# Retention: the left-over keys' low parts behind the corner scores, the first head's key copies outside of the scores, the second copy of high parts on ScalarE

## The chip, the cores and the metric

The kernel runs on one core of a Trainium2 chip. A core has a matrix engine (TensorE; PE in the profile, with its weight loads PEld), a vector engine (VectorE, DVE), an engine for activations (ScalarE, ACT), a general one (GpSimd, POOL) and a queue engine (SyncE, SP). They run side by side and wait for each other by semaphores. The metric is the time of one execution on the device in microseconds.

## The reference

One transformer block in float32 on 512 tokens of width 1024, with 16 learned tokens (`meta`) put in front, so 528 positions: a feed-forward part, a mixer and a second feed-forward part, each on an RMS-normed input and added to the residual. The mixer projects the input to everything it needs at once, and adds a retention branch (4 heads, keys of 256, values of 512) and an attention branch (8 heads that attend to 128 keys picked by an index score), each with its own gate. The retention, which the change is about, multiplies scores by a decay that depends on the distance of query and key:

```python
inner = jnp.einsum('bhqk,bhke->bhqe', jnp.einsum('bhqd,bhkd->bhqk', qc, kc) * d_in, vc)
cross = jnp.einsum('bhqd,bhde->bhqe', qc, state) * xi
state = g_chunk * state + jnp.einsum('bhkd,bhke->bhde', kc * zeta, vc)
```

In the reference it runs in chunks of 128 with a state. The kernel computes the same as one causal product over all 528 positions.

## The kernel before

Every large product is float32 carried by three products of rounded parts: an operand is split in a high part (a rounded copy, made by ScalarE) and a low part (what is left, a subtraction on VectorE), and high x high, high x low and low x high are added up in PSUM. `in_two` makes the high part at once and returns a function that makes the low part later, so the program decides where in VectorE's queue it stands. Weights (`raw`) become `whi` and `wlo` in the same way.

The order of the work of PE, ScalarE and VectorE is written out by hand here: each engine executes its instructions in the order in which the Python code issues them, and a waiting instruction holds up all behind it on its engine. Tiles come from pools with a fixed number of places (four places for `tmp`); a new tile takes a place whose former reader may still be at work, and then its first write waits for that reader.

The retention of a head h: `decayed(h)` scores all queries against four blocks of 128 keys (`psst`, kb = 0 to 3; PE), multiplies each by the decay (L1837: VectorE, from PSUM to `tmp`) and splits it in `ph` and `pl`. Queries start at position 16 and keys at 0, so the last 16 queries of each block of 128 also meet 16 keys beyond that block of keys, the left-over keys: these small squares of scores are the corners. `corner_keys()` copies those keys next to each other (L1826, two VectorE copies to a `tmp` tile, "CAST" in the profile), `corners(h)` has PE score them in six small matmuls, multiplies them by the decay (L1854), and places the result in `ptail` three times: the high part (L1860, ScalarE), the low part (L1861, VectorE), and the high part again (L1862, GpSimd). The left-over keys' values stand in `vtail` in the same way: `split_last(h)` makes the high parts on ScalarE (L1635 or L1638) and returns the function of the low part (L1639, VectorE). `weigh(h, b)` then adds up for each block of queries the weighted values of all key blocks (`pspv`, L1874), and in one further matmul those of the left-over keys (L1875, called the tail matmul here).

Head 0 runs between gate and query projections: its scores follow the second gate tile, and the corners stand inside the projection of head 1's queries (`psrq`), at its fifth of eight steps. `split_last(0)` and its low part are issued at the second step. Heads 1 to 3 run inside the output projection of the head before (`psro`, `outputs`, four steps of two halves): step 0 splits the left-over values' high parts, step 1 makes their low part and the values' own parts (`values_in`: high by ScalarE, two low parts by GpSimd, L1774), step 2 runs the scores, step 3 the corners between its halves, and then the weighing. Copies of `psro` go through ScalarE (L2019, L2022), and from head 2 on GpSimd adds them up (L2023).

Of the kernel before, what the change touches and what calls it, by code (L numbers as in the profile page):

```python
# [11 lines left out]
F32 = mybir.dt.float32  # L12
F32R = mybir.dt.float32r
AF = mybir.ActivationFunctionType
# [69 lines left out]
def kernel(ctx: ExitStack, tc: tile.TileContext, x, meta, g1, wg1, wu1, wd1, gm,  # L84
                      w_in, w_ro, w_ao, w_mo, g2, wg2, wu2, wd2, gf, rope, decay, causal, out):
    nc = tc.nc
# [1596 lines left out]
    if True:  # L1683
# [145 lines left out]
        def decayed(h):  # L1829
            rk, u = ret_k, heads[h]["u"]  # L1830
            prob, low = [], lambda: None
            for kb in range(4):
                n = S - kb * P
                ps = sm_tile("psst")[:, :n]
                scored(ps, [[t[:, kb * P : (kb + 1) * P] for t in rk[k]] for k in range(2)], lambda t: t[:, kb * P :])
                t = tmp()[:, :n]
                TT(t, ps, u[0][:, :n], ALU.mult)  # L1837
                low()
                ph = rt.tile([P, n], F32R, tag=f"ph{kb}", name="ph")
                pl = rt.tile([P, n], F32R, tag=f"pl{kb}", name="pl")  # L1840
                low = in_two(t, ph, pl)
                prob.append((ph, pl))
                if kb == 1:
                    corner_keys()
            low()
            heads[h]["prob"] = prob

        def corners(h):

            last_k, u = corner["k"], heads[h]["u"]  # L1850
            ps = sm_tile("psst")[:NT, :NT]
            scored(ps.rearrange("p (b q) -> p b q", q=NM), [[last_k[:, 2 * j + i].rearrange("p b q -> p (b q)") for j in range(2)] for i in range(2)], lambda t: t.rearrange("p (b q) -> p b q", q=P)[:, :, P - NM :])
            t = tmp()[:NT, :NT]
            TT(t, ps, u[1], ALU.mult)  # L1854
            last = tp["p"].rearrange("p (a b q) -> p a b q", a=2, q=P)
            for a in range(2):
                at = slice(a * 2 * NM, (a + 1) * 2 * NM)
                src = t[at, at].rearrange("p (b q) -> p b q", q=NM)
                h_, l_, again = (last[i * 2 * NM : (i + 1) * 2 * NM, a, :, P - NM :] for i in range(3))
                nc.scalar.activation(h_, src, AF.Copy)  # L1860
                TT(l_, src, h_.bitcast(F32), ALU.subtract)  # L1861
                nc.gpsimd.tensor_copy(again, h_.bitcast(F32))  # L1862

        def weigh(h, b):

# [40 lines left out]
        def fetch_turned(h, half):  # L1906
            t = heads[h]["land", half] = room4("land")
            nc.sync.dma_start(t.rearrange("p a b -> p (a b)").rearrange("p (k e) -> p k e", k=4),
                              ots[h % 2, half].rearrange("(k p) a e -> p k (a e)", p=P))
# [62 lines left out]
        def queries_keys(h, asides, inside=((), (), (), ())):  # L1972

            pss = {}
            ropes = heads[h]["ropes"] = {}

            def q0(ps):
                pss["qa"] = ps
                asides[0]()

            def q1(ps):
                pss["qb"] = ps
                ropes["q"] = rope_pieces(pss["qa"], ps, cos[:, REAL], sin[:, REAL], S, ret_q)
                asides[1]()
                some(ropes["q"], 5)

            def k0(ps):
                pss["ka"] = ps
                asides[2]()
                some(ropes["q"], 2)  # L1990

            def k1(ps):
                ropes["k"] = rope_pieces(pss["ka"], ps, cos, sin, T, ret_k)
                asides[3]()

            return (steps_of(tiles(("rq", h), w_in, OFF_RQ + h * DK, 2), [proj("psrq", REAL, inside[0], q0), proj("psrq", REAL, inside[1], q1)])
                    + steps_of(tiles(("rk", h), w_in, OFF_RK + h * DK, 2), [proj("psrk", None, inside[2], k0), proj("psrk", None, inside[3], k1)]))

        def outputs(h, beside):

            def step(i):
                def run(w, lower):
                    if h == 0 and i == 0:
                        ixs.close()
                        ap = mx["acc"] = accs.enter_context(pool("acc", 1, side="right"))
                        acc_r.extend(ap.tile([P, S], F32, tag=f"accr{c}", name=f"accr{c}") for c in range(KD))
                        vr["pool"] = vrs.enter_context(pool("vraw", 1, side="right"))
                    if i == 0 and h + 1 < RH:
                        fetch_head(h + 1)
                        new_decay(h + 1)  # L2010
                    elif i == 0:
                        vr["raw"] = fetch_values(0, vraw()[:, :1024])
                    for j in range(2):
                        ps = sm_tile("psro")
                        mm3([(ps, slice(0, S))], [t[:, :, j * P : (j + 1) * P] for t in w],
                            lambda k: [t[:, k, :] for t in heads[h]["o"]], DV // P)
                        a = acc_r[2 * i + j]
                        if h == 0:
                            nc.scalar.activation(a, ps, AF.Copy)  # L2019
                        else:  # L2020
                            t = RR[:, j * S : (j + 1) * S]
                            nc.scalar.activation(t, ps, AF.Copy)  # L2022
                            nc.gpsimd.tensor_tensor(a, a, t, ALU.add)  # L2023
                        if j == 0:
                            lower()
                            if i == 3 and h + 1 < RH:
                                corners(h + 1)
                            beside(i)
                    if h + 1 < RH:
                        if i == 0:  # L2030
                            heads[h + 1]["last"] = split_last(h + 1)
                        if i == 1:
                            heads[h + 1]["last"]()
                            values_in(h + 1)
                        if i == 2:
                            decayed(h + 1)
                        if i == 3:
                            weigh_all(h + 1)
                return run

            return steps_of(tiles(("ro", h), w_ro[h * DV : (h + 1) * DV, :], 0, 4, DV // P, 2 * P), [step(i) for i in range(4)])
# [72 lines left out]
        gr = tiles("gr", w_in, OFF_GR, 7)  # L2114
        more = steps_of(gr[:2], [start_0, start_1])
        nothing = lambda: None
        more += queries_keys(1, (beside_q0, beside_q1, lambda: fetch_turned(0, 1), nothing), (((1, lambda: split_last(0)()), (4, lambda: corners(0))), (), ((3, lambda: (index_queries(4), index_keys(2))), (5, first_pairs)), ((6, pair),)))
        come = [(i, lambda half=half: arrived(0, (half,))) for half, i in enumerate((1, 5))]
        more += steps_of(gr[2:4], [proj("psgate", REAL, (*come, *((i, pair) for i in (2, 4, 6, 7))), later_gate(2)),
                                   proj("psgate", REAL, tuple((i, pair) for i in (1, 3, 5, 6, 7)), after_3)])  # L2120
# [922 lines left out]
    pair = []  # L3043
# [83 lines left out]
```

## Time and profile before

| what | us |
|---|---|
| median of 3 runs (lowest to highest) | 1493.6 (1492.47 to 1494.25) |
| the profiled execution | 1492.96 |
| its span, from first to last instruction | 1491.2 |
| PE busy | 1463.7 (98%) |
| VectorE busy | 1164.0 (78%) |
| ScalarE busy | 784.1 (53%) |
| GpSimd busy | 296.9 (20%) |

How to read the rows shown below. A row of the timeline has the start in us from the span's start, the duration in us, the engine, the line of the kernel, the operation, what it writes and reads, the shape, the number of instructions merged, and in brackets how long the engine stood idle before it and what ended that. A row of the waits has the waiting engine and line, what it waited for, the total in us, how many times, and the longest. A row of the groups has the busy time in us, and the mean of one instruction in ns. A row of the windows has a stretch, its length, the busy time of PE, PEld, DVE, ACT and POOL in it with the number of instructions, the clock granted to TensorE (1.00 is full speed), the share of the DMA engines, and GB/s. An instruction's duration can hold a wait for something that both it and another engine use, since such a wait comes after its start.

### The profile page before, as it was taken

Reading aid. Unit: us, or ns where it says so; the run is one execution under the profiler, and the core shown is the slowest. Engines: PE = TensorE matmul, PEld = TensorE weight load, DVE = VectorE, ACT = ScalarE, POOL = GpSimd, SP = SyncE. Lnnn points to the kernel's source line nnn. Section 1 sums busy time; section 2 is a strip of 40 time slices with the busy share of each in tenths; the row PEclk is TensorE's granted clock in tenths of the full one; section 3 lists DMA queues with packets and bytes.
Section 4 is the critical chain, followed back from the end, with each engine's and each line's share of the span. In section 5 each row is a group of like instructions: output and inputs, shape, how many; then the busy total and the mean of one; then the engine's idle time right before and its main releaser. Section 6 shows DMA issues by size and latency. Waiting matters only on the chain.

```text
span 1491.2 us, 22544 instructions
## 1 busy us (share of the span) xinstructions
PE 1463.7 (98%) x8626; PEld 1291.2 (87%) x8626; DVE 1164.0 (78%) x1702; ACT 784.1 (53%) x1122; POOL 296.9 (20%) x381
## 2 busy tenths in 40 slices
PE   9999999999999999989989999999999999999998
PEld 8999999999988888777878788888888888888887
DVE  5998898866887987478788798889657787767676
ACT  6656465454354554556444547777534644434344
POOL 1101111102111000321142532444202321211110
PEclk9999999999999999999999999999999999999999
DMA  5458787556554452744436343866746576466423
GB/s 172 111 155 198 181 186 190 142 132 228 199 168 144 163 169 112 228 140 157 124 121 202 95 156 97 232 173 177 247 154 228 155 236 202 130 209 189 136 77 122
DMA packets 210333, 247.36 MB, mean 166 GB/s; under 512 B 32208, under 2 KB 153928, under 8 KB 210224
## 3 DMA queue, kind: packets, MB, share of 16 engines
q1 hardware_dynamic: 171824, 179.77, 37.8%
q0 software_dynamic: 34480, 59.30, 16.3%
q10 hardware_dynamic: 3920, 6.84, 1.4%
q8 instruction: 68, 1.11, 0.3%
q14 instruction: 41, 0.34, 0.1%
HBM read 206.47 MB, written 39.21 MB: 165 GB/s over the span
## 4 chain that ended last, share of the span: by engine, by line
PE 92%; DVE 3%; DMA 2%; ACT 1%; issue 1%; ACTq 0%; DVEq 0%; SPq 0%; POOL 0%; POOLq 0%
PE psd L2852 8%; PE psvX L1445 7%; PE psqX L2685 7%; PE psqX L162 7%; PE psqZ L162 5%; PE psd L162 4%; PE psqY L2685 4%; PE psvY L1445 4%; PE psro L162 3%; PE psak L162 3%; PE psrk L162 3%; PE psaq L162 3%; PE psga L162 3%; PE psat L162 3%; PE psmo L162 3%; PE psgate L162 3%
## 5 line engine op out<-in xcount | busy, mean ns | idle before, releaser
L330 DVE TENSOR_TENSOR wlo<-raw,whi 128x1024 fp32r<-128x1024 f32 (+2 forms) x138 | 159.3, 1156 | 36.3 <-ACT whi L329 35.2
L329 ACT ACTIVATE whi<-raw 128x1024 fp32r<-128x1024 f32 (+2 forms) x138 | 130.0, 943 | 84.2 <-PE psat L162 9.4
L330 DVE TENSOR_TENSOR wlo<-w,whi 128x1024 fp32r<-128x1024 f32 x96 | 116.9, 1219 | 62.2 <-ACT whi L329 62.0
L329 ACT ACTIVATE whi<-w 128x1024 fp32r<-128x1024 f32 x96 | 101.6, 1058 | 103.1 <-PE psd L2852 39.3
L162 PE MATMUL psro<-o,whi 128*128 128x512 f32 x256 | 83.3, 408 | 0.0
L329 ACT ACTIVATE whi<-wsum 128x1024 fp32r<-128x1024 f32 (+1 forms) x48 | 48.3, 1007 | 39.7 <-issue 11.8
L119 ACT ACTIVATE whi<-raw 128x1024 fp32r<-128x1024 f32 (+1 forms) x43 | 43.7, 1016 | 36.2 <-PE psat L162 9.1
L120 DVE TENSOR_TENSOR wlo<-raw,whi 128x1024 fp32r<-128x1024 f32 (+1 forms) x43 | 52.7, 1228 | 9.7 <-ACT whi L119 9.5
L162 PEld LDWEIGHTS psro<-o,whi 128*128 128x128 f32 x256 | 50.1, 199 | 10.3
L2648 POOL DMA_DIRECT2D hts<-cross x40 | 26.1, 660 | 165.1 <-DVE cross L2645 144.1
L2852 PE MATMUL psd<-wlo,hh 128*128 128x512 f32 (+1 forms) x148 | 56.7, 383 | 0.0
L2852 PE MATMUL psd<-whi,hl 128*128 128x512 f32 (+1 forms) x148 | 56.7, 383 | 0.0
L2852 PE MATMUL psd<-whi,hh 128*128 128x512 f32 (+1 forms) x148 | 56.7, 383 | 0.0
L330 DVE TENSOR_TENSOR wlo<-wsum,whi 128x1024 fp32r<-128x1024 f32 (+1 forms) x48 | 55.2, 1152 | 1.4 <-ACT whi L329 1.0
L162 PE MATMUL psro<-o,wlo 128*128 128x512 f32 x128 | 51.8, 404 | 0.0
L2023 POOL TENSOR_TENSOR accr<-accr,RR 128x512 f32<-128x512 f32 x24 | 35.6, 1488 | 71.9 <-ACT RR L2022 71.8
L1445 PE MATMUL psvX<-wlo,th 128*128 128x512 f32 x120 | 46.8, 390 | 0.0
L1445 PE MATMUL psvX<-whi,tl 128*128 128x512 f32 x120 | 46.7, 389 | 0.0
L1445 PE MATMUL psvX<-whi,th 128*128 128x512 f32 x120 | 46.7, 389 | 0.0
L162 PE MATMUL psqX<-xh,wlo 128*128 128x264 f32 x144 | 40.9, 284 | 1.1 <-DVE wlo L330 1.1
L162 PE MATMUL psqZ<-xh,wlo 128*128 128x264 f32 x144 | 40.8, 283 | 0.0
L162 PE MATMUL psqX<-th,whi 128*128 128x264 f32 x144 | 40.8, 283 | 0.0
(635 smaller groups left out, 5048.8 us busy)
## 6 DMA issues: line engine op xcount, KB each, us to landing
w<-in_w_in_dram SPq DMA_DIRECT2D x40, 512.0 KB, 4.6
raw<-in_w_in_dram SPq DMA_DIRECT2D x27, 512.0 KB, 3.9
raw<-in_w_in_dram SPq DMA_DIRECT2D x13, 1024.0 KB, 6.1
raw<-in_ffn_w_down_dram SPq DMA_DIRECT2D x24, 512.0 KB, 4.2
raw<-in_ffn_w_up_dram SPq DMA_DIRECT2D x11, 1024.0 KB, 5.3
raw<-in_ffn_w_gate_dram SPq DMA_DIRECT2D x10, 1024.0 KB, 5.4
ws<-in_ffn_w_up_dram POOLq DMA_DIRECT2D x20, 512.0 KB, 6.2
w<-in_ffn_w_up_dram SPq DMA_DIRECT2D x20, 512.0 KB, 5.4
```

The lines of the kernel that those rows point to most:

```text
L119: nc.scalar.activation(hi, src, AF.Copy)
L120: eng.tensor_tensor(lo, src, hi.bitcast(F32), ALU.subtract)
L162: nc.tensor.matmul(o, a[:, k, :], b[:, sl], start=first and k == 0 and i == 0, stop=last and k == nk - 1 and i == 2, skip_group_check=onto)
L329: nc.scalar.activation(hi, src, AF.Copy)
L330: return lambda: nc.vector.tensor_tensor(lo, src, hi.bitcast(F32), ALU.subtract)
L1445: nc.tensor.matmul(d[bank_][t], a, b[:, k, :], start=not onto and j + k + m == 0, stop=j + k == 3 and m == 2, skip_group_check=onto)
L2023: nc.gpsimd.tensor_tensor(a, a, t, ALU.add)
L2648: nc.gpsimd.dma_start(d.rearrange("(b i) a e -> a i b e", i=32)[a], cross[32 * a : 32 * a + 32].rearrange("p b c t -> p b (c t)"))
L2685: nc.tensor.matmul(ps[:, t], a, b[:, k, :], start=not onto and j + k + m == 0, stop=j + k == 3 and m == 2, skip_group_check=onto)
L2852: nc.tensor.matmul(ps, a, m[:, j, cs], start=first and i == 0, stop=last and i == 2)
```

## The change

Three edits, all in the retention's bookkeeping of the left-over keys. What is computed stays the same.

```diff
@@ decayed(h)
                 prob.append((ph, pl))
-                if kb == 1:
+                if kb == 1 and h:
                     corner_keys()
@@ corners(h)
                 nc.scalar.activation(h_, src, AF.Copy)
+                nc.scalar.activation(again, src, AF.Copy)
                 TT(l_, src, h_.bitcast(F32), ALU.subtract)
-                nc.gpsimd.tensor_copy(again, h_.bitcast(F32))
+            heads[h].pop("last")()
@@ outputs(h, beside), step i
                         if i == 1:
-                            heads[h + 1]["last"]()
                             values_in(h + 1)
@@ the query projection of head 1, steps 1 and 4 of its first tile
-((1, lambda: split_last(0)()), (4, lambda: corners(0)))
+((1, lambda: (corner_keys(), heads[0].update(last=split_last(0)))), (4, lambda: corners(0)))
```

First, head 0's keys are copied after all its scores, no longer between the second and the third block. Second, the copy of the high part that GpSimd made from ScalarE's first copy is made by ScalarE from the source. Third, the low part of `vtail` is made at the end of `corners(h)`, in head 0 too. From L1861 on, lines after the change have a number that is one higher.

VectorE in head 0, from the second block's product on: the piece of the difference around the scores.

```order
 L1837 TENSOR_TENSOR tmp<-psst,RR 128x384
 L330 TENSOR_TENSOR pl<-tmp,ph 128x512
-L1826 CAST tmp<-rqk 128x4x48
-L1826 CAST tmp<-rqk 128x4x16
 L1837 TENSOR_TENSOR tmp<-psst,RR 128x256
 L330 TENSOR_TENSOR pl<-tmp,ph 128x384
```

The two copies of the keys no longer stand ahead of the third block's product (128x256). They come behind the values' second low part:

```order
 L330 TENSOR_TENSOR pl<-tmp,ph 128x128
 L1774 TENSOR_TENSOR vl<-vl,vh 128x1024
+L1826 CAST tmp<-rqk 128x4x48
+L1826 CAST tmp<-rqk 128x4x16
+L1854 TENSOR_TENSOR tmp<-psst,ulast 64x64
+L1862 TENSOR_TENSOR ptail<-tmp,ptail 32x2x16 x2
 L1639 TENSOR_TENSOR vtail<-vtail 32x1024
-L1854 TENSOR_TENSOR tmp<-psst,ulast 64x64
-L1861 TENSOR_TENSOR ptail<-tmp,ptail 32x2x16 x2
```

Here the corners' product and low parts also changed places with the low part of `vtail`. VectorE in head 1, whose scores begin behind a weight's low part (`wlo`) and a selection step (MAX, MATCH_REPLACE); heads 2 and 3 read the same:

```order
 L1599 MAX top<-score_6522 128x8
 L1600 MATCH_REPLACE score_6522<-top,score_6522 128x512
-L1639 TENSOR_TENSOR vtail<-vtail 32x1024
 L330 TENSOR_TENSOR wlo<-raw,whi 128x1024
 L1837 TENSOR_TENSOR tmp<-psst,RR 128x512
...
 L1854 TENSOR_TENSOR tmp<-psst,ulast 64x64
-L1861 TENSOR_TENSOR ptail<-tmp,ptail 32x2x16 x2
+L1862 TENSOR_TENSOR ptail<-tmp,ptail 32x2x16 x2
+L1639 TENSOR_TENSOR vtail<-vtail 32x1024
```

The low part left its place ahead of `wlo` and the scores and stands behind the corners' low parts, as the last thing that the tail matmul needs. The order of PE's instructions and of the loads issued by SyncE is unchanged.

## Prediction before the result

> **What bounds the kernel now.** I read the page's first part and its chain, then TensorE's (PE's) own waits.
>
> ```profile
> span 1491.2 us, 22544 instructions
> PE 1463.7 (98%) x8626; PEld 1291.2 (87%) x8626; DVE 1164.0 (78%) x1702; ACT 784.1 (53%) x1122; POOL 296.9 (20%) x381
> PE psst L1818 <- DVE tmp L1837: 11.0, 3, 4.5
> PE pspv L1875 <- POOL ptail L1862: 6.7, 1, 6.7
> ```
>
> PE sets the time, so work elsewhere counts only where PE waits. It waits in two places worth anything, both in the retention, both touched by the change: once 6.7 us in the first head (head 0), and three times, 11.0 us together, in heads 1 to 3. Each wait costs twice, as the stretches with their granted clock show (start:end, length, busy us of PE, PEld, DVE, ACT, POOL, then PEclk).
>
> ```profile
> 182.42:185.83 3.41, 2.31 (x20) 2.10 (x18) 1.97 (x3) 1.06 (x1) 0.00 (x0) 1.00 0.68 114
> 704.65:708.06 3.41, 0.64 (x6) 0.64 (x6) 3.18 (x3) 2.03 (x4) 1.03 (x1) 1.00 0.00 0
> 708.06:711.48 3.42, 3.42 (x11) 2.74 (x10) 2.72 (x9) 2.07 (x4) 0.00 (x0) 0.50 0.00 0
> 637.96:643.21 5.25, 5.25 (x12) 4.12 (x13) 2.62 (x5) 1.49 (x4) 0.13 (x1) 0.50 0.01 4
> 769.50:776.33 6.83, 5.73 (x17) 4.77 (x18) 5.90 (x12) 2.72 (x5) 2.81 (x2) 0.50 0.00 1
> 834.36:837.77 3.41, 3.41 (x10) 2.65 (x9) 3.13 (x8) 1.28 (x3) 0.69 (x1) 0.50 0.84 289
> ```
>
> After each long wait PE runs at half clock for 3.4 or 6.8 us; half of PE's busy time there is lost: 2.6, 1.7, 2.9, 1.7 us. A stretch of 3.41 us with PE idle for 1.1 of it (182.42) was followed by no slow one; one with 2.77 idle (704.65) was.
>
> **Head 0: the keys copied later.** Before, in order of time:
>
> ```profile
> 624.50 0.39 DVE L1826 CAST tmp<-rqk 128x192 fp32r<-128x192 f32 x2
> 627.26 0.43 PE L1818 MATMUL psst<-rqk,tmp 128*64 128x64 f32 x5
> 627.77 0.43 DVE L1837 TENSOR_TENSOR tmp<-psst,RR 128x256 f32<-128x256 f32 x1 [2.88 <-PE psst L1818]
> 630.65 2.00 ACT L1784 ACTIVATE g<-g 128x1024 f32<-128x1024 f32 x2
> 632.56 1.04 ACT L329 ACTIVATE whi<-raw 128x1024 fp32r<-128x1024 f32 x1
> 633.61 2.12 ACT L1638 ACTIVATE vtail<-vtail 32x1024 fp32r<-32x1024 f32 x2
> 635.76 1.22 DVE L1639 TENSOR_TENSOR vtail<-vtail 32x1024 fp32r<-32x1024 f32 x1 [4.32 <-ACT vtail L1638]
> 637.01 0.22 DVE L1854 TENSOR_TENSOR tmp<-psst,ulast 64x64 f32<-64x64 f32 x1
> 637.96 0.80 PE L1875 MATMUL pspv<-vtail,ptail 96*128 96x512 f32 x1 [6.71 <-POOL ptail L1862]
> ```
>
> The third product with the decay (627.77) starts only when the corner matmuls that read the copied keys are through: its `tmp` takes the place of that copy. ScalarE's whole row of work, up to the high parts of the left-over keys' values (ending 635.73), hangs behind it. With the copy after the scores, the product starts where the CAST stood, near 624.5. I take 3.2 us of the 3.27 for all of ScalarE's row, as nothing in it is shown waiting for a load. From the end of `vtail`'s high parts to PE's tail matmul it was 2.23. Now it is the four small copies and their low parts (about 1.0, priced below), then the low part of `vtail`, 1.22: the same 2.2, since the corner product (0.22) now lies ahead of ScalarE's copies. The tail matmul starts near 634.75: **3.2 earlier**. The two CASTs now follow four small products and low parts and one `vl`, together about 3.2 us, so the corner matmuls wait to about 628.2, 1 us later than before. That is hidden: PE still reaches the tail near 632.1 and waits there until 634.75. Without that cover it would cost 1 us.
>
> **Heads 1 to 3: the low part moved.** Head 1:
>
> ```profile
> 699.92 2.41 POOL L1774 TENSOR_TENSOR vraw<-vraw,vh 128x1024 fp32r<-128x1024 f32 x1 [13.50 <-ACT vh L1771]
> 702.31 3.37 POOL L1774 TENSOR_TENSOR vraw<-vraw,vh 128x1024 fp32r<-128x1024 f32 x1
> 700.58 2.84 DVE L1639 TENSOR_TENSOR vtail<-vtail 32x1024 fp32r<-32x1024 f32 x1
> 703.62 3.15 DVE L330 TENSOR_TENSOR wlo<-raw,whi 128x1024 fp32r<-128x1024 f32 x1 [0.20 <-DVE vtail L1639]
> 705.44 0.58 ACT L2019 ACTIVATE accr<-psro 128x512 f32<-128x512 f32 x1
> 707.40 0.63 ACT L329 ACTIVATE ph<-tmp 128x512 fp32r<-128x512 f32 x1 [1.38 <-DVE tmp L1837]
> 707.42 0.33 PE L1818 MATMUL psst<-rqk 128*128 128x128 f32 x1 [3.08 <-DVE tmp L1837]
> 711.35 1.23 DVE L330 TENSOR_TENSOR wlo<-raw,whi 128x1024 fp32r<-128x1024 f32 x1 [0.66 <-ACT whi L329]
> 716.37 0.40 PE L1875 MATMUL pspv<-vtail,ptail 96*128 96x512 f32 x1
> ```
>
> The low part takes 1.22 in head 0 and 2.84 here, `wlo` 1.23 or 3.15. The ends say why: the low part ends 1.1 after the first GpSimd subtraction, the second one ends 2.26 after the low part, `wlo` 1.1 after that. Two engines take turns here, one instruction at a time. Without the low part, `wlo` takes its turn (702.25 to 703.45), and the score product that frees PE's bank follows at 703.4, not 706.7, if it need not take turns itself:
>
> ```profile
> 768.82 2.26 POOL L2023 TENSOR_TENSOR accr<-accr,RR 128x512 f32<-128x512 f32 x1
> 769.86 0.68 DVE L1837 TENSOR_TENSOR tmp<-psst,RR 128x512 f32<-128x512 f32 x1
> 771.03 1.28 POOL L2023 TENSOR_TENSOR accr<-accr,RR 128x512 f32<-128x512 f32 x1
> 771.24 1.61 DVE L330 TENSOR_TENSOR pl<-tmp,ph 128x512 fp32r<-128x512 f32 x1 [0.23 <-ACT ph L329]
> L1837 DVE TENSOR_TENSOR tmp<-psst,RR 128x512 f32<-128x512 f32 x4 | 2.7, 682 | 2.2 <-PE psst L1818 2.2
> ```
>
> It does not: 0.68 beside a GpSimd addition, and 682 ns is the mean of all four. `pl`, with both inputs in SBUF, does (1.61).
>
> So PE's wait of 3.08 at 707.42 and its slow stretch go. But they don't all become time: what was moved is late next. ScalarE's `ph` can't start before its copy ends at 706.02, so the run from `ph` to the end of the second `wlo` (707.40 to 712.58, 5.18) ends at 711.2. Behind it stand the corner product (0.22), the four copies with their low parts (1.0) and now the moved low part (1.22): the tail's operand is ready near 713.6. PE, at full clock from 704.34, needs 716.37 - 707.42 - 1.7 = 7.25 and is there at 711.6. New wait 2.0; the tail starts at 713.6 instead of 716.37, **2.8 earlier**.
>
> Heads 2 and 3 differ: GpSimd also has two additions of 1.28 queued behind its subtractions, and DVE's keys' CASTs come now between them.
>
> ```profile
> L1826 DVE CAST tmp<-rqk 128x192 fp32r<-128x192 f32 x4 | 1.0, 252 | 0.0
> L1826 DVE CAST tmp<-rqk 128x64 fp32r<-128x64 f32 x4 | 0.8, 191 | 0.0
> L1860 ACT ACTIVATE ptail<-tmp 32x32 fp32r<-32x32 f32 x8 | 1.8, 229 | 2.0 <-DVE tmp L1854 1.9
> 772.78 0.35 DVE L1826 CAST tmp<-rqk 128x192 fp32r<-128x192 f32 x2
> 835.52 0.35 DVE L1826 CAST tmp<-rqk 128x192 fp32r<-128x192 f32 x2
> 780.64 0.40 PE L1875 MATMUL pspv<-vtail,ptail 96*128 96x512 f32 x1
> 842.25 0.40 PE L1875 MATMUL pspv<-vtail,ptail 96*128 96x512 f32 x1
> ```
>
> No row shows a CAST beside a GpSimd instruction, so its price is between 0.35 and 0.35 + 2 x 1.28 for the pair. It takes 61 ns for 128 more elements, where the product takes 682 for 512: a faster way of running, so I price it like the nearest row that waits, `pl`, as taking turns: the pair then ends near 772.1 in head 2 (before 773.1) and 835.0 in head 3 (before 835.9). The corner matmuls wait about 1.7 in both. Everything behind follows by 1.0 and 0.9 earlier, then the low parts meet one more addition, and the low part of `vtail` ends near 778.6 and 841.4: tails **2.0** and **0.85 earlier**. If CASTs don't take turns, each is 1.5 better.
> [...]
>
> **The second copy.** Eight GpSimd copies go, eight on ScalarE come, 0.23 each by the L1860 row (the same shape and source); the 0.5 per head is inside the 1.0 above. They delay ScalarE's next copy of `psro`, which waits for PE anyway. The low part delays one selection step by 1.2 us on DVE; its next job waits for PE's first weighted sum.
>
> **The sum.** Tails: 3.2 + 2.8 + 2.0 + 0.85 = 8.85. Clock: the losses of heads 1 to 3 lie before their tails and are in these; head 0's 2.6 lies behind its tail and goes too. Against that stand the new waits ahead of the four tails, 2.0 to 2.75 us: between the 1.1 that cost nothing and the 2.77 that did, nearer to the latter. Each may cost 0 to 1.7; I take 1.0, so 4.0. Net 8.85 + 2.6 - 4.0 = 7.4. The profiled execution took 1492.96, its span and 1.76 around it; so 1485.5 for it, and 1486 beside the median of 1493.6.
>
> **Rivals.**
> *No new slow stretch*, because a wait must fill a whole 3.4 us: the 4.0 falls away, 1482. For it: 1.1 us idle cost nothing. Against it: 2.77 of 3.41 sufficed.
> [...]
> *CASTs take no turns*: 3.0 better, 1483.
> *The stall merely moves in heads 1 to 3*: if the chain to the low part ends where PE arrived before (2.8, 2.0, 0.85 later than I work out, say through more turns lost to additions), only 3.2 + 2.6 - 4.0 = 1.8 is left: 1491.8, no change. For it: the low part is now the last link of its chain in every head.
> *Head 0's edit does nothing*, because the third product waits for another reader of `tmp`: 5.65 - 3.0 = 2.7, 1491. Against it: the 2.88 ends exactly with the corner matmuls.
> *Slower, by the clock*: one long stall becomes two shorter ones (seven in all: corner and tail in heads 0, 2 and 3, the tail in head 1). If 1 to 1.7 us idle is enough for a slow stretch, and the four long ones give two each as at 769.50, it is 3 x 1.7 + 4 x 2.75 = 16.1 against 11.45: 4.6 slower, 1498. It decides where such a short wait slows PE at all; the 182.42 row, at 1.1, speaks against it.
>
> **How the numbers follow.** Forecast 0.50, no new slow stretch 0.15, CASTs 0.12, stall moves 0.10, head 0 nothing 0.08, slower 0.05. A measurement tells 0.2%, 3.0 us, from no change. Faster: the first three and a few parts of the fifth, 0.80; same 0.15; slower 0.05. The forecast's own range runs from four waits at no cost (1482) to four at 1.7 (1488.8), with 1 us of turns more, 1490. With the cheaper CASTs below and part of the moved stall above: 1480 to 1491.
>
> **What would show it.** Right: PE's wait on L1837 down from 11.0 us to under 2; waits of 2 to 3 us at the tail matmul behind the low part in all heads; the third product of head 0 near 624.5; L1639 at 1.2 us; `ph` in head 1 straight behind a `psro` copy. Wrong: L1837 still late behind a GpSimd subtraction; CASTs at 0.35 beside additions; PE waiting for weights or loads where it did not before; half clock after waits under 1.5 us.

## The result, and the profile after

The changed kernel takes 1483.7 us (median of 6 runs, 1481.85 to 1486.41), beside 1493.03 for the kernel before on the same chip. The ratio is 0.9943, with a 95% interval of 0.9925 to 0.9962: 8.5 us less, 6 to 11 by the interval. The profiled execution is the slowest of the six, 1486.41, with a span of 1484.6. A second profile of the same kernel, taken later beside the experiments, has a span of 1483.9.

The page's first part, after the change:

```profile
span 1484.6 us, 22535 instructions
...
PE 1462.5 (99%) x8626; PEld 1288.9 (87%) x8626; DVE 1155.0 (78%) x1702; ACT 785.5 (53%) x1130; POOL 298.3 (20%) x373
```

PE's waits after the change (engine and line, what ended the wait, total us, times, longest):

```profile
PE pspv L1876 <- ACT RR L2023: 4.3, 2, 2.2
PE pspv L1876 <- POOL bias L1595: 3.0, 1, 3.0
PE psst L1818 <- DVE tmp L1826: 2.7, 3, 1.1
PE pspv L1876 <- ACT accr L2020: 1.8, 1, 1.8
PE psS L2271 <- ACT ak L329: 1.3, 1, 1.3
...
PE psst L1818 <- DVE tmp L1837: 0.5, 1, 0.5
```

The 11.0 us at L1837 are down to 0.5. The 6.7 at head 0's tail matmul became four waits at the tail matmuls (L1876 now), 3.0, 1.8 and twice 2.2: 9.1 together. The names of what ended them mislead: in the timeline the low part of `vtail` (L1639) ends 0.1 to 0.2 us ahead of each tail matmul, later than anything else that it reads.

The timeline of the changed kernel, head 0:

```profile
623.52 0.42 DVE L1837 TENSOR_TENSOR tmp<-psst,RR 128x256 f32<-128x256 f32 x1
...
626.52 0.36 DVE L1826 CAST tmp<-rqk 128x192 fp32r<-128x192 f32 x2
626.94 0.54 PE L1818 MATMUL psst<-rqk,tmp 128*64 128x64 f32 x6 [0.58 <-DVE tmp L1826]
...
629.43 2.13 ACT L1638 ACTIVATE vtail<-vtail 32x1024 fp32r<-32x1024 f32 x2
...
632.35 0.18 DVE L1862 TENSOR_TENSOR ptail<-tmp,ptail 32x32 fp32r<-32x32 f32 x1 [0.32 <-ACT ptail L1860]
632.56 1.22 DVE L1639 TENSOR_TENSOR vtail<-vtail 32x1024 fp32r<-32x1024 f32 x1
...
633.99 0.47 PE L1876 MATMUL pspv<-vtail,ptail 96*128 96x512 f32 x1 [2.98 <-POOL bias L1595]
```

The third product (623.52) no longer has a wait ahead of it, ScalarE's high parts of `vtail` end at 631.55 and not at 635.73, and the tail matmul is now bound by ScalarE's four small copies and VectorE's low parts behind them.

Head 1, and behind it head 2 (whose GpSimd rows at L2024 are the additions):

```profile
700.62 0.58 ACT L2020 ACTIVATE accr<-psro 128x512 f32<-128x512 f32 x1
701.09 1.03 ACT L329 ACTIVATE ph<-tmp 128x512 fp32r<-128x512 f32 x2
...
705.03 1.22 DVE L330 TENSOR_TENSOR wlo<-raw,whi 128x1024 fp32r<-128x1024 f32 x1 [0.66 <-ACT whi L329]
...
707.40 1.22 DVE L1639 TENSOR_TENSOR vtail<-vtail 32x1024 fp32r<-32x1024 f32 x1
...
708.72 0.47 PE L1876 MATMUL pspv<-vtail,ptail 96*128 96x512 f32 x1 [1.83 <-ACT accr L2020]
...
761.62 2.99 POOL L2024 TENSOR_TENSOR accr<-accr,RR 128x512 f32<-128x512 f32 x2
762.15 2.52 DVE L1826 CAST tmp<-rqk 128x192 fp32r<-128x192 f32 x2
...
764.81 0.51 PE L1818 MATMUL psst<-rqk,tmp 128*64 128x64 f32 x6 [1.06 <-DVE tmp L1826]
...
769.64 1.22 DVE L1639 TENSOR_TENSOR vtail<-vtail 32x1024 fp32r<-32x1024 f32 x1
...
770.96 0.69 PE L1876 MATMUL pspv<-vtail,ptail 96*128 96x512 f32 x1 [2.15 <-ACT RR L2023]
```

In head 1, `ph` stands right behind a copy of `psro`, and the low part of `vtail` takes 1.22, where it took 2.84. In head 2 the two CASTs take 2.52 us beside two additions; before they took 0.35.

The granted clock behind the waits, in windows of the changed kernel:

```profile
706.19:709.60 3.41, 1.58 (x8) 1.02 (x7) 2.69 (x8) 1.89 (x6) 0.00 (x0) 1.00 0.00 0
709.60:713.02 3.42, 3.42 (x10) 2.64 (x9) 1.65 (x3) 1.11 (x4) 0.00 (x0) 0.50 0.02 5
...
767.63:771.04 3.41, 1.26 (x7) 0.75 (x6) 3.02 (x6) 1.51 (x5) 2.70 (x2) 1.00 0.01 2
771.04:774.46 3.42, 3.42 (x9) 2.65 (x10) 1.99 (x4) 0.80 (x2) 0.96 (x1) 0.50 0.00 0
829.07:832.48 3.41, 1.50 (x7) 0.92 (x5) 3.05 (x5) 1.64 (x6) 2.49 (x2) 1.00 0.00 0
832.48:835.89 3.41, 3.17 (x14) 2.64 (x15) 2.28 (x6) 1.49 (x4) 1.29 (x1) 1.00 0.00 0
972.43:975.84 3.41, 1.91 (x10) 1.18 (x9) 2.44 (x6) 1.93 (x4) 0.07 (x1) 1.00 0.86 247
975.84:979.26 3.42, 3.42 (x15) 3.16 (x14) 3.42 (x12) 3.37 (x4) 0.51 (x1) 0.50 0.24 85
```

Half clock follows the tail waits of heads 1 and 2 (709.60, 771.04), and likewise that of head 0. It does not follow head 3's wait (832.48) in this profile; in the second one it does, at 832.15. A new half-clock stretch (975.84) lies in the attention, some 140 us behind the last changed instruction.

Where the time went is best seen by cutting the span at PE's own rows. "To the tail" runs from a head's first score matmul (L1818) to its first tail matmul, "weighing" from there to its fourth tail matmul, and "attention" from its first score matmul (`psS`) to its first output matmul (`psmo`); all are us, differences of two starts.

| stretch | before | changed | changed, second profile | only the keys' copies moved | only the low part moved | only the second copy |
|---|---|---|---|---|---|---|
| head 0 to the tail | 17.26 | 14.34 | 14.35 | 14.07 | 18.07 | 18.03 |
| weighing | 9.42 | 8.54 | 8.54 | 8.52 | 8.52 | 8.49 |
| head 1 to the tail | 15.31 | 12.49 | 12.49 | 16.72 | 12.23 | 16.79 |
| weighing | 6.96 | 8.59 | 8.60 | 6.96 | 7.02 | 6.96 |
| head 2 to the tail | 18.30 | 14.64 | 14.69 | 15.66 | 15.91 | 15.93 |
| weighing | 6.96 | 8.57 | 8.58 | 6.96 | 8.57 | 6.96 |
| head 3 to the tail | 15.64 | 14.18 | 14.14 | 15.83 | 14.67 | 15.57 |
| weighing | 6.96 | 7.02 | 8.59 | 6.96 | 7.03 | 6.96 |
| attention | 205.16 | 207.27 | 206.09 | 205.18 | 205.05 | 204.73 |

The tails came 2.92, 2.82, 3.66 and 1.46 earlier, 10.86 in all. A weighing of 8.5 to 8.6 instead of 6.96 is one with a half-clock stretch. The attention, which nothing in the diff touches, took 2.1 and 0.9 us longer in the two profiles of the changed kernel.

The last three columns belong to the experiments. They also show how far one profile can be trusted: in the two kernels that leave the order of VectorE's work in heads 1 and 2 as it was (keys' copies, second copy) head 1 to the tail differs from before by +1.4 and +1.5, and head 2 by -2.6 and -2.4. The double half-clock stretch (6.83 us, at 769.50 before) fell in head 1 and not in head 2, and a turn that VectorE lost to GpSimd ahead of head 2's scores before (a `wlo` of 2.16 us) was not lost there (1.22). Sums over all heads, and the timed ratios, carry the argument.

### The profile page after: what moved, and what is told of

The parts are those of the page before. It is cut to its first block, busy times and chain, and to the rows that moved or that the text cites. A ratio compares the mean times of both kernels' runs of the same rounds, so it can differ in the third digit from the quotient of the medians.

```text
span 1484.6 us, 22535 instructions
## 1 busy us (share of the span) xinstructions
PE 1462.5 (99%) x8626; PEld 1288.9 (87%) x8626; DVE 1155.0 (78%) x1702; ACT 785.5 (53%) x1130; POOL 298.3 (20%) x373
## 4 chain that ended last, share of the span: by engine, by line
PE 88%; DVE 4%; ACT 3%; DMA 3%; issue 1%; POOL 0%; SPq 0%; DVEq 0%; ACTq 0%; POOLq 0%
PE psd L2852 8%; PE psqX L2685 7%; PE psvX L1445 7%; PE psqX L162 7%; PE psqZ L162 5%; PE psd L162 4%; PE psqY L2685 4%; PE psvY L1445 4%; PE psrk L162 3%; PE psat L162 3%; PE psmo L162 3%; PE psak L162 3%; PE psrq L162 3%; PE psdX L162 2%; PE psaq L162 2%; PE psga L162 2%
## 5 line engine op out<-in xcount | busy, mean ns | idle before, releaser
L330 DVE TENSOR_TENSOR wlo<-raw,whi 128x1024 fp32r<-128x1024 f32 (+2 forms) x138 | 154.7, 1123 | 39.6 <-ACT whi L329 38.9
L330 DVE TENSOR_TENSOR wlo<-w,whi 128x1024 fp32r<-128x1024 f32 x96 | 116.8, 1219 | 62.1 <-ACT whi L329 61.9
L162 PE MATMUL psro<-o,whi 128*128 128x512 f32 x256 | 79.4, 391 | 0.0
L330 DVE TENSOR_TENSOR wlo<-wsum,whi 128x1024 fp32r<-128x1024 f32 (+1 forms) x48 | 55.2, 1152 | 1.4 <-ACT whi L329 1.0
L2024 POOL TENSOR_TENSOR accr<-accr,RR 128x512 f32<-128x512 f32 x24 | 37.9, 1581 | 64.1 <-ACT RR L2023 64.0
L162 PE MATMUL psqX<-th,wlo 128*128 128x264 f32 x144 | 40.7, 283 | 0.0
```

The costliest lines, as they stand in the source:

```text
L162: nc.tensor.matmul(o, a[:, k, :], b[:, sl], start=first and k == 0 and i == 0, stop=last and k == nk - 1 and i == 2, skip_group_check=onto)
L330: return lambda: nc.vector.tensor_tensor(lo, src, hi.bitcast(F32), ALU.subtract)
```

## The experiments

### The change once more, and its three parts one by one

The changed kernel again, with no edit:

> The change itself beside its three parts. Theory (the edits act at different places): its gain is the sum of the three parts' within 3 us, 7 to 11 us. Rival (the parts need each other): it gains over 3 us more than their sum.

Measured: 0.9943 (0.9927 to 0.996), the same ratio as at first, 1485.5 us beside 1493.2, some 8.5 us by the ratio and so in the range expected. The stretches to the tails are the same to 0.05 us (the table); the half clock behind head 3's appeared here and not in the first profile.

Only the keys' copies of head 0 moved (against the kernel before):

```diff
-                if kb == 1:
+                if kb == 1 and h:
                     corner_keys()
-((1, lambda: split_last(0)()), (4, lambda: corners(0)))
+((1, lambda: (corner_keys(), split_last(0)())), (4, lambda: corners(0)))
```

> Only head 0's keys are copied after its scores; the low part stays at its old place and GpSimd keeps the second copy. Theory (the third product waited for the corner matmuls through the place in tmp): that product starts some 0.1 us after the first low part, the 6.7 us wait at head 0's tail matmul falls to 3 to 3.5, the 11.0 us at L1837 in heads 1 to 3 stay; 3.2 of the tail and 0 to 1.7 of the clock come off: 2 to 5 us faster than before. Rival (the gain at head 0 needs the low part's move or ScalarE's second copy): the wait stays above 5 us, under 1 us faster.

Measured: 0.996 (0.9945 to 0.9975), 6.0 us, where 2 to 5 were expected. Its PE waits, and the third product:

```profile
PE psst L1818 <- DVE tmp L1837: 10.1, 3, 3.6
PE pspv L1875 <- POOL ptail L1862: 2.7, 1, 2.7
...
624.71 0.42 DVE L1837 TENSOR_TENSOR tmp<-psst,RR 128x256 f32<-128x256 f32 x1
```

The third product starts 3.9 us after the head's first score (620.83), where it started 7.1 after (620.70 and 627.77). Head 0's wait fell from 6.7 to 2.7 (3 to 3.5 expected), its tail came 3.19 earlier (17.26 to 14.07), and heads 1 to 3 kept their 10 us. So the place of a `tmp` tile in head 0, not the values' high parts, held up ScalarE's whole row; the rival that head 0's edit does nothing falls.

Only the low part of `vtail` moved:

```diff
                 nc.gpsimd.tensor_copy(again, h_.bitcast(F32))
+            heads[h].pop("last")()
-                            heads[h + 1]["last"]()
                             values_in(h + 1)
-((1, lambda: split_last(0)()), (4, lambda: corners(0)))
+((1, lambda: heads[0].update(last=split_last(0))), (4, lambda: corners(0)))
```

> Only the low part of vtail is moved behind the corners, in all heads. Theory (the low part cost a turn ahead of the weight's low part and the first product): PE's wait at L1837 falls from 11.0 us to under 2, head 0 keeps its 6.7 us, and the tail matmuls of heads 1 to 3 now wait 1.8 to 2.7 us each; 5.65 us earlier tails less up to 1.7 of slow clock each: 1 to 5.5 us faster. Rival (the stall only moves): waits of 3 us or more at the tails, within 1 us of before.

Measured: 0.9959 (0.9943 to 0.9975), 6.1 us, where 1 to 5.5 were expected. Its PE waits:

```profile
PE pspv L1876 <- issue: 13.2, 4, 7.5
...
PE psst L1818 <- DVE tmp L1837: 1.6, 2, 1.2
```

The wait at the scores fell from 11.0 to 1.6, and the tails' waits in heads 1 to 3 are 1.62, 1.85 and 2.21. In heads 1 and 3 this is all of the change's effect but some 0.5 (12.23 and 14.67 to the tail, beside 12.49 and 14.18). In head 2 the tail came at 15.91 and not 14.64. In head 0 the wait grew from 6.7 to 7.5, but not by the low part's new place: from the end of `vtail`'s high parts to the tail it is 2.1 us, where it was 2.23. A `pl` of VectorE (L330 at 629.71), right behind the third product, took 1.52 beside a GpSimd instruction that had been waiting for a load (L1733 at 629.53); before, the same `pl` took 0.55 and started just ahead of that instruction (628.12 and 628.16).

Only the second copy on ScalarE:

```diff
                 nc.scalar.activation(h_, src, AF.Copy)
+                nc.scalar.activation(again, src, AF.Copy)
                 TT(l_, src, h_.bitcast(F32), ALU.subtract)
-                nc.gpsimd.tensor_copy(again, h_.bitcast(F32))
```

> Only the second copy of the high parts goes from GpSimd to ScalarE. Theory: nothing that PE waits for moves, waits of 11.0 and 6.7 us stay within 0.5, time within 1.5 us of before. Rival (0.5 us more on ScalarE per head is on the path): head 0's wait 0.3 to 0.5 us longer, 0.5 to 2 us slower; rival (GpSimd's copy was the last link, as the wait names it): 0.5 to 1 us faster in head 0.

Measured: 0.9998 (0.9984 to 1.0011). No difference can be measured. PE waits 10.2 us at L1837, and 7.5 ahead of head 0's tail; that is 0.8 more than before, where at most 0.5 was expected, but not by the copies: from the end of `vtail`'s high parts to the tail it is 2.13 beside 2.23, and the same `pl` as in the kernel above lost a turn (1.42). The weighing behind it was 0.9 shorter (8.49 for 9.42), and the two stretches together are no longer than before (26.5 and 26.7).

The parts alone give 6.0, 6.1 and 0.3, 12.4 together, and the change 8.5; the sum was expected to come within 3 us. With intervals of some 2 us on each of the four the gap of 3.9 is not clear of noise, but the two profiles of the change show where such a gap may lie. All three weighings behind the tails of heads 1 to 3 can carry half clock there (1.6 each), where the low part alone shows it once; and the attention lost 0.9 to 2.1 in them alone.

### What the four new waits hang on

Each of the next three kernels adds one edit to the changed kernel. The copies of the keys of heads 1 to 3 by ScalarE:

```diff
+                if h:
+                    nc.scalar.activation(do, of.bitcast(F32), AF.Copy)
+                else:
                     nc.vector.tensor_copy(do, of.bitcast(F32))
```

> The changed kernel, but the copies of heads 1 to 3's keys (the CASTs) are made by ScalarE in place of VectorE; nothing is left out. Theory (a CAST takes 1.3 us in heads 2 and 3 because it takes turns with GpSimd's additions, 1.1 us each, and PE's corner matmuls wait for it): the copies last under 0.4 us beside the additions, PE's corner waits of 1.06 and 1.08 us vanish or fall under 0.4, the two tails start 1 to 2 us earlier, and the time is 1 to 3 us below the changed kernel's, 1481 to 1484.5. Rival (the CASTs are only late, since the scores and their high parts end late): the copies on ScalarE start as late as the CASTs ended, the corner waits stay at 1 us or more, and the time is within 1 us of the changed kernel's.

Measured: 0.992 (0.9905 to 0.9935), 3.4 us better than the change by the ratios, with intervals that just overlap. Head 2 (in this kernel L1827 is the copy, L2027 the additions):

```profile
758.44 0.50 ACT L1827 ACTIVATE tmp<-rqk 128x192 fp32r<-128x192 f32 x2
759.00 3.31 POOL L2027 TENSOR_TENSOR accr<-accr,RR 128x512 f32<-128x512 f32 x2
...
760.99 0.48 PE L1818 MATMUL psst<-rqk,tmp 128*64 128x64 f32 x6
```

The pair takes 0.50 on ScalarE, where it took 2.52 on VectorE, PE no longer waits for the corners, and the tails of heads 2 and 3 come 1.6 and 1.7 earlier (13.06 and 12.49). So the CASTs' turns with GpSimd set the corner waits. The tail waits stayed, at 1.6 to 1.8 in heads 1 to 3.

The corners ahead of the weight's second low part, and the low part of `vtail` ahead of `ptail`'s:

```diff
             TT(t, ps, u[1], ALU.mult)
+            heads[h].pop("last")()
 ...
                 TT(l_, src, h_.bitcast(F32), ALU.subtract)
-            heads[h].pop("last")()
 ...
                         if j == 0:
-                            lower()
                             if i == 3 and h + 1 < RH:
                                 corners(h + 1)
+                            lower()
```

> The changed kernel with the low part of vtail issued right behind the corners' product, ahead of ptail's low parts, and with the corners issued ahead of the weight's second low part (wlo); nothing is left out. Theory (the tail matmul waits because three things in a row end late: wlo 1.2 us, ptail's parts, and vtail's low part 1.2 us): the tail's wait in head 1 falls from 1.8 to under 0.6, in heads 2 and 3 from 2.15 to 1.0 or less, tails of heads 1 to 3 start 1 to 2 us earlier each, one or more of the slow stretches behind them go; 1478 to 1482. Rival (wlo is needed at once by PE): the wait reappears as long in a PE wait for wlo behind the tail or in the projection, and the time stays within 1 us of 1485.

Measured: 0.989 (0.9873 to 0.9907), 7.9 us better than the change. Head 2 (L1863 is `ptail`'s low part here):

```profile
761.76 1.22 DVE L1639 TENSOR_TENSOR vtail<-vtail 32x1024 fp32r<-32x1024 f32 x1
...
763.09 2.34 DVE L1863 TENSOR_TENSOR ptail<-tmp,ptail 32x32 fp32r<-32x32 f32 x2
...
764.27 0.47 PE L1876 MATMUL pspv<-vtail,ptail 96*128 96x512 f32 x1 [0.42 <-ACT RR L2023]
```

The tail's wait is gone in head 1, 0.42 in head 2 and 0.2 in head 3, with no wait for `wlo` in its place; the weighings of heads 1 to 3 are 6.96, 7.02 and 7.02, without half clock. This is the largest gain of the three kernels: ahead of the tail's last links stood `wlo`, which nobody needed yet. Its two moves were not run apart, and a score product in head 3 now waits 1.2 where it did not.

Head 0's gate step (a table load and two activations) behind the corners:

```diff
             heads[0]["low"](1)
-            open_gates(0)
 ...
-(4, lambda: corners(0))
+(4, lambda: (corners(0), open_gates(0)))
```

> The changed kernel with the first head's gate step (a load of the activation table and two ACTIVATEs, 3.3 us of ScalarE) issued behind the corners, no longer ahead of the high parts of vtail; nothing is left out. Theory (ScalarE's row alone sets the end of head 0's tail): the wait of 2.98 us ahead of head 0's tail falls under 0.5, the tail starts 2.5 to 3 us earlier, the slow stretch behind it (1.5 us lost) goes; 4 us below the changed kernel, 1480 to 1482. Rival (VectorE's row sets it: CASTs, corner product, low parts): the wait only falls to 1.5 to 2.5 us and the slow stretch stays; 1484 to 1485.5.

Measured: 0.9922 (0.9906 to 0.9937), 3.1 us better than the change, again with intervals that just overlap. Head 0:

```profile
629.04 1.22 DVE L1639 TENSOR_TENSOR vtail<-vtail 32x1024 fp32r<-32x1024 f32 x1
...
630.61 0.40 PE L1876 MATMUL pspv<-vtail,ptail 96*128 96x512 f32 x1
```

No wait is left ahead of head 0's tail, which comes 3.2 earlier than in the changed kernel (14.34 to 11.16), and its weighing is at full clock (6.83 for 8.54). ScalarE's row alone set that tail.

### All three together, and what is left

The last three edits in one kernel, run twice, on two chips:

> The three edits before together: key copies of heads 1 to 3 on ScalarE, vtail's low part and the corners ahead of wlo, the first head's gate step behind the corners; nothing is left out. Theory (each takes a wait of its own, and the slow stretches go with the waits): no PE wait over 1 us is left in the retention, and the time is the sum of the three, 8 to 12 us below the changed kernel: 1473 to 1478. Rival (the waits are one chain, or the gain goes to another wait in the attention that follows): less than 5 us below, 1481 or more.

> The version with all three edits once more, beside the three runs before it on the same chip. Expected: a ratio of 0.987 to the kernel before, within 0.002, and a profile with the same waits (1.2 twice at the score products); which heads show half clock may differ, since the same wait was followed by half clock in one execution and not in another.

Measured: 0.9868 (0.9851 to 0.9886) and 0.9858 (0.9839 to 0.9878): some 20 us below the kernel before, and faster than the changed kernel by more than the intervals. The longest group of waits in the retention, from the first run (L1840 is the score product):

```profile
PE psst L1818 <- DVE tmp L1840: 2.4, 2, 1.2
```

No wait over 1.2 us is left in the retention (none over 1.0 was expected), and one half-clock stretch, in head 3, behind a window of 3.41 us with waits of 0.3 and 1.2 in it. The edits alone are worth 3.4, 7.9 and 3.1 over the change, 14.4 together; in one kernel they give 11 to 13. Part of this need not be an overlap of the edits: in each of their three profiles the attention takes 204.5 to 205.6 us and in the two of the change 206.1 and 207.3, and that difference counts three times in the 14.4. The next run tests one of the edits for overlap.

The same without the keys' copies on ScalarE:

> The three edits together but without the key copies on ScalarE (they stay on VectorE); nothing is left out. Theory (once vtail's low part stands ahead, the tail no longer hangs on the corners, so a CAST's turn of 1.1 us costs PE only the corner wait of 1.0 in heads 2 and 3): corner waits of about 1.0 and 1.0 return, the waits for the score product (1.2 each) shrink or stay, and the time is within 1.5 us of the version with all three (about 1473). Rival (the gains of the edits add): 3 us above the version with all three, 1476 or more.

Measured: 0.9863 (0.9847 to 0.9879), beside 0.9858 for all three on the same chip: no difference can be measured. In this profile the corner waits of 1.05 and 1.03 are back, and one of the two waits of 1.2 at the score products is gone. Once the tail no longer hangs on the corners, a corner wait of 1 us mostly takes the place of another one.

The weight's low part of the third output step behind the second score product (added to all three):

```diff
                 TT(t, ps, u[0][:, :n], ALU.mult)
+                if kb == 1:
+                    weight()
                 low()
 ...
-                            lower()
+                            if i != 2 or h + 1 == RH:
+                                lower()
                             beside(i)
 ...
-                            decayed(h + 1)
+                            decayed(h + 1, lower)
```

> The version with all three edits, and the weight's low part (wlo) of the third output step issued behind the second score product, no longer ahead of the first; nothing is left out. Theory (the two waits of 1.2 us that are left in heads 2 and 3 are the first product queued behind wlo, which takes turns with GpSimd's subtraction for 2.0 us): both vanish or fall under 0.3, the corner and tail matmuls start about 1 us earlier in heads 2 and 3, and the time falls by 2 to 4 us to 1469 to 1471. Rival (wlo is then late for PE's next output matmuls): a wait of 0.5 to 1.5 us for wlo in heads 1 to 3 takes their place, and the time stays within 1 us or rises.

Measured: 0.9861 (0.9839 to 0.9883), no gain over 0.9858, where 2 to 4 us were expected; the rival had the time right and the wait wrong. The two waits of 1.2 did go, and PE did not wait for `wlo` in the retention, but in head 2 this came instead (L1868 is `ptail`'s low part, L2029 the additions, L1881 the tail):

```profile
760.03 3.32 POOL L2029 TENSOR_TENSOR accr<-accr,RR 128x512 f32<-128x512 f32 x2 [0.90 <-ACT RR L2028]
761.10 2.31 DVE L1868 TENSOR_TENSOR ptail<-tmp,ptail 32x32 fp32r<-32x32 f32 x2
...
762.26 0.47 PE L1881 MATMUL pspv<-vtail,ptail 96*128 96x512 f32 x1 [1.74 <-ACT RR L2028]
```

`ptail`'s two low parts (0.18 each alone, L1862 in head 0 above) took turns with two additions and lasted 2.31, and the tail waited 1.74 again, and 0.98 in head 3.

The same with the keys' copies back on VectorE:

> As the run before, but with the key copies of heads 1 to 3 on VectorE; nothing is left out. Theory (CASTs take turns with the additions, so the corner waits of about 1 us return in heads 2 and 3): 1 to 3 us above the run before. Rival (with the products earlier, the CASTs come before the additions and take no turn): under 0.5 us per pair and the same time as the run before within 1 us.

Measured: 0.9889 (0.9869 to 0.9908), 4.2 us worse than the kernel before it in this list by the two ratios (1 to 3 expected), though the intervals overlap. Head 2:

```profile
757.14 1.41 DVE L1826 CAST tmp<-rqk 128x192 fp32r<-128x192 f32 x2
...
758.70 0.63 PE L1818 MATMUL psst<-rqk,tmp 128*64 128x64 f32 x6 [1.86 <-DVE tmp L1826]
```

Only one CAST of the pair lost a turn here, but the low parts ahead of it had lost theirs (a `wlo` of 2.48 us, a `pl` of 1.77), and the corner waits are 1.86 and 1.69, each followed by half clock. Of the kernels run, the one with all three edits is the best, with the two before this one no different within the noise; the order of VectorE's work beside GpSimd's additions is what is left to arrange.

## Why the prediction was right, point by point

**The sum.** Forecast 1486.0, measured 1483.7; the profiled run was put at 1485.5 and took 1486.41. The time alone does not tell the forecast from the rivals at 1482 and 1483; the profiles do, with slow stretches behind the new waits and CASTs that take turns. The mechanisms are those forecast, but the terms erred in both directions, and that they cancelled is luck. In the profiled spans: tails 10.86 earlier (8.85 predicted); clock -2.42 (0.9 gained in head 0's weighing, 1.63, 1.61 and 0.06 lost in the others; -1.4 predicted from 2.6 and 4.0); the attention and the rest -2.96 (2.11 in the attention; nothing predicted); and 1.06 from a start of the retention that was earlier in this execution. 10.86 - 2.42 - 2.96 + 1.06 = 6.54, the difference of the spans (1491.17 - 1484.63), where 7.4 was predicted. The second profile gives 10.84 - 4.01 - 1.36 + 1.82 = 7.29. The earlier start is not the change's: before, PE waited 1.1 us for a weight at 185.75, more than 430 us ahead of the first changed instruction, and in the two profiles of the change it did not; in the profiles of its three parts it did, 1.1 to 2.1.

**Head 0.** Right in mechanism and size. The third product starts 3.2 earlier once the start's shift of 1.06 is taken off (627.77 to 623.52), and the tail 2.92, not 3.2: the way from the high parts of `vtail` to the tail is 2.44 us (631.55 to 633.99), not 2.2, since the fourth copy and both low parts stand in a row. The corner matmuls' later start (628.0 on the clock of before, predicted 628.2) was hidden, as said. The slow stretch went from 6.8 to 3.4 us, so the clock's net gain of 1.6 (2.6 less 1.0) was 0.9.

**Head 1.** Right to 0.1: counted from the first score the tail comes at 12.49, where the forecast's rows give 12.5 (713.6 - 701.06), and the wait is 1.83 (2.0). That it is 2.82 earlier (2.8) hangs on the one profile before; beside the two other kernels with the old order it is 4.2 and 4.3 earlier, since they had a double half-clock stretch there.

**Heads 2 and 3.** The CASTs take turns, as priced against the cheaper case: 1.34 and 1.26 us beside the additions, where they took 0.18 to 0.26 before. No row of before had a CAST beside a GpSimd addition, so the price, taken from `pl` (1.61), was an estimate. On ScalarE the pair takes 0.50 beside the same additions. Beside the profile before, the sizes were off: the corner waits are 1.06 and 1.08, not 1.7, and the tails 3.66 and 1.46 earlier, not 2.0 and 0.85. The step that was mis-sized is where the pair of CASTs ends. Counted from the head's first score matmul (762.34 before, 756.31 after), head 2's pair ends 2.4 us earlier (773.13 before, 764.66 after), and 1.0 was predicted; from there to the tail it is 6.3, where 6.5 was predicted. I had left GpSimd's additions where they were. But the first one starts 5.3 us after the first score and not 6.5 (768.82 before, 761.62 after), and the CASTs' turns come that much sooner. The cause lies further back, 12.5 us ahead of head 2's scores, in a `wlo` that lost a turn to an addition before and not after:

```profile
749.83 2.16 DVE L330 TENSOR_TENSOR wlo<-raw,whi 128x1024 fp32r<-128x1024 f32 x1
```

```profile
743.52 1.22 DVE L330 TENSOR_TENSOR wlo<-raw,whi 128x1024 fp32r<-128x1024 f32 x1
```

After, it starts 0.28 us earlier beside PE's scores, and all rows of VectorE, ScalarE and GpSimd from there to the additions stand 1.2 earlier. This does not go with the edit: with the keys' copies alone and with the second copy alone, which leave the order there as it was, that `wlo` took 1.22 too, and with the low part alone it took 2.13. Beside those two profiles with the old order head 2's pair ends 0.9 and 1.2 earlier, as predicted, and its tail 1.0 and 1.3. So 2.0 lies between what these and the profile before give, and how much of the 3.66 belongs to the change stays open. In head 3, where all three profiles of the old order agree to 0.3, the pair ends 1.4 earlier in place of 0.9, and the tail 1.4 to 1.7 in place of 0.85: there the term was too low.

**The second copy.** Zero, as predicted; the run with it alone gives 0.3 us, with an interval of some 2 us to either side.

**The new waits' clock.** This term was mis-sized. I took 1.0 for each of the four. Half clock followed three of them in one profile and all four in the other, at about 1.6 each, near the upper bound of 1.7.

**What was not foreseen.** A wait in the attention. Before and after, at the same place:

```profile
976.92 0.68 DVE L1554 TENSOR_TENSOR tmp<-tmp 128x512 f32<-128x512 f32 x1
977.38 1.41 POOL L1551 TENSOR_TENSOR tmp<-tmp,sin 128x528 f32<-128x528 f32 x1
977.52 2.35 DVE L120 TENSOR_TENSOR wlo<-raw,whi 128x1024 fp32r<-128x1024 f32 x1
```

```profile
967.95 2.36 DVE L1554 TENSOR_TENSOR tmp<-tmp 128x512 f32<-128x512 f32 x1
968.41 1.35 POOL L1551 TENSOR_TENSOR tmp<-tmp,sin 128x528 f32<-128x528 f32 x1
...
974.50 0.45 PE L2271 MATMUL psS<-ak,aq 128*128 128x400 f32 x1 [1.34 <-ACT ak L329]
```

Before, VectorE's sum (L1554) is through in 0.68 and the instruction behind it waits for GpSimd; after, the sum itself waits, everything behind it is later, and PE waits 1.34 for the attention's keys (0.5 before), with half clock behind. The lag between the two engines is 0.46 us in both. The sum waits in both profiles of the changed kernel (2.36 and 2.35; PE's wait in the second is 1.2, with no half clock behind it) and in none of the kernels with one part alone. Of the eight later profiles, all of kernels that contain the change, one has it: the three edits without the copies on ScalarE (2.35, PE's wait 1.2, no half clock). Why the turn goes the other way here was not settled, nor whether it does in every execution.

**The rivals.** No new slow stretch: fell, three and four of the waits had one, in the first profile behind windows of 3.41 us with 1.83 to 2.89 idle. CASTs without turns: fell. The stall merely moves in heads 1 to 3: fell, the low part alone gives 6.1 us. Head 0's edit does nothing: fell, it alone gives 6.0. Slower by the clock: fell by the time, and no corner wait of 0.6 to 1.1 in the changed kernel was followed by half clock; but its condition, that 1 to 1.7 us idle can be enough, was met in the attention (1.50 idle in the window at 972.43).

**The signs named.** All five for "right" appeared: L1837 at 0.5, tail waits of 1.8 to 3.0 (2 to 3 named), the third product at 623.52, L1639 at 1.22 in all four heads, `ph` behind a copy. One sign for "wrong" did too: half clock behind a wait of 1.34 in the attention (975.84).

## What to carry to other kernels

When a stalled step is moved behind other work, its new place has a chain of its own, and the last link decides: here a weight's low part that nobody needed yet and a gate's activations stood ahead of it, and putting these behind was worth more than the change itself. VectorE and GpSimd, which took turns in these rows, should be ordered by who waits for them, small instructions included: a CAST of 0.18 to 0.26 us before took 1.26 or 1.34 beside a GpSimd addition after, and which instruction pays can differ from one profile to the next of the same order, as with the `wlo` ahead of head 2. In these profiles PE's idle time of up to 1.37 us within one window of 3.41 us was not followed by half clock; 2.02 us and more was, which made a weighing 1.6 us longer (8.57 for 6.96 in head 2), and short waits in one window add up: 0.3 and 1.2 us were followed by it in the kernel with all three edits. A wait in one profile should be looked for in other kernels that leave its place alone before it is put down to an edit.

## What the runs showed of the hardware

**The half-clock stretches started on a grid of 3.413 us, and 1.50 us of PE idle in one window of it could be enough.** In the 13 profiles that have more than one, the starts of the half-clock stretches lie whole multiples of 3.413 us apart (in the changed kernel 634.51, 709.60, 771.04 and 975.84: 22, 18 and 60 windows), with another offset in each run (before, the first one starts at 636.38). Taking PE's idle time in each window of that grid, over the 14 profiles of this case, from 100 to 1400 us, and without the windows that are at half clock themselves: up to 1.37 us idle was never followed by half clock, 2.02 and more always was (21 times); between 1.42 and 1.93 it was 11 times and 9 times not. Before, the windows at 182.42 (1.10 idle) and 629.56 (1.72) were not followed by half clock, those at 830.94 (2.38) and 704.65 (2.77) were; after, those at 972.43 (1.50), 706.19 (1.83) and 631.10 (2.89) were. So the same wait of 2.15 was followed by half clock where it lay in one window (767.63 to 771.04 in the changed kernel) and not where an edge cut it in 1.91 and 0.24 (832.48). The window at 972.43 had PE busy for 1.91 of its 3.41 us. What decides between 1.4 and 2.0 us stays open: the window at 829.07 with 1.91 idle was not followed by half clock, the one at 706.19 with 1.83 was.

**The order of starts does not always show who gets the turn.** With the `wlo` ahead of head 2's scores the one that started first was through first: before, it started 0.21 us behind an addition of 1.29 (749.62) and took 2.16; after, it started 0.08 ahead of one (743.60), took 1.22, and the addition took 2.30. In the attention rows above VectorE's sum starts 0.46 us ahead of GpSimd's product both times; before, it was through first, at 977.60 for 978.79, and after, it ended at 970.31, 0.55 behind GpSimd (969.76).
